# Three blocks per channel-tile pair for the float32 products of a chunked scan among float32r projections

## The chip, the cores and the metric

One Trainium2 chip, one of its cores. The metric is the device time of one execution in microseconds (us). The kernel before was run three times: 1105.64, 1105.64 and 1105.79 us, median 1105.64.

## What is computed

One layer of a streaming encoder on 512 tokens of 1024 numbers: an input layer norm, a mixing layer with two branches (a chunked state-space scan, and top-k attention over shared latents), and a gated convolutional feed-forward layer. The change is in the scan branch. Cut to that, the reference is:

```python
def _ssd_scan(X, a, Bm, Cm):
    ...
    a_cum = jnp.cumsum(a.astype(jnp.float32), axis=-1)
    seg = a_cum[..., :, None] - a_cum[..., None, :]
    decay = jnp.exp(jnp.where(causal, seg, -jnp.inf))
    cb = jnp.einsum('bclgn,bcsgn->bgcls', Cm, Bm)
    y_diag = jnp.einsum('bgecls,bcsgep->bclgep', cb[:, :, None] * decay, X)
    decay_states = jnp.exp(a_cum[..., -1:] - a_cum).transpose(0, 3, 4, 1, 2)
    states = jnp.einsum('bclgn,bclgep->cbgepn', Bm, X * decay_states[..., None])
    ...
    _, prev = lax.scan(step, init, (states, chunk_decay))
    y_off = jnp.einsum('bclgn,cbgepn->bclgep', Cm, prev) * \
        jnp.exp(a_cum).transpose(0, 3, 4, 1, 2)[..., None]
    return (y_diag + y_off).reshape(Bsz, L, H, P)

def _ssd_branch(z, xbc, dt, conv_w, conv_b, dt_bias, A_log, D_skip, norm_g):
    xbc = jax.nn.silu(_causal_dwconv(xbc, conv_w, conv_b))
    ...
    y = _ssd_scan(xs * dt[..., None], dt * A, Bm, Cm)
    y = (y + xs * D_skip[:, None]).reshape(Bsz, L, SSD_INNER)
    v = (y * jax.nn.silu(z)).astype(jnp.float32).reshape(Bsz, L, SSD_GROUPS, SSD_INNER // SSD_GROUPS)
    v = v * lax.rsqrt(jnp.mean(v * v, -1, keepdims=True) + LN_EPS)
    return (v.reshape(Bsz, L, SSD_INNER) * norm_g).astype(z.dtype)
```

The branch has 4 groups of B and C with 128 states each, and 2048 channels. Everything is float32.

## The kernel before

**Two kinds of products on PE (TensorE).** The large projections are exact to about float32 by splitting both factors into a high and a low float32r half: a step is three matmuls, high by high, high by low, low by high, of 128x512 outputs (`mm3`, recorded at L215). A projection of one tile of 128 output channels takes 8 such steps, one per 128 input channels (`steps`, L267), and accumulates in one of three PSUM buffers `acc`. The weights come by DMA on SP's queue into `wraw`; ACT makes `whi` (L188), DVE makes `wlo` (L189). The scan's own products are plain float32 matmuls and transposes of smaller shapes, also recorded at L215 and L218; they write the PSUM banks a, b and c (one buffer each: `pa`, `pb`, `pc` in the profile) and `ptr` (two buffers, `tr_tile`, L111).

**The scan, per group g and channel tile j (128 channels, two heads), L665 to L797.** 

- `ssd_b` transposes B into `bt`, `ssd_cb` multiplies C and B per chunk of 128 tokens into `ptr`, and DVE masks that into `cbm` (both once per group).
- `ssd_x` issues three DMAs (the logs of decay G, two halves of `eaB`), transposes the convolved x into `ptr` (4 transposes), and DVE evicts it twice, as `xdd` (x times dt and decay) and `xd` (x times dt), L702 and L703.
- `ssd_g`, four times per tile, turns G into decays on ACT; `ssd_gm` multiplies G by `cbm` on DVE (L720).
- `ssd_s` makes the states of three chunks (3 products) in bank a or b; ACT and DVE run them through the chunks (`pv`, L735).
- `ssd_y` multiplies C with these states (3 products), DVE multiplies by `eaB` (L747).
- `ssd_d` makes the products within chunks for two tiles (8 products each); DVE (L762), POOL (L763) and the gate add up v.
- After four tiles `ssd_root` sums the squares on PE, `ssd_norm` (four transposes, then DVE at L795) scales v and splits it into `yhi` and `ylo` (L175), the input of the output projection `out_br`.

**The order of the work** around the change is written by hand. `run(projs, items)` (L835) steps through a list of projections and records behind step k the items listed under k; `pair` (L845) makes such a list for two channel tiles from a tuple of steps: x0, x1 (`ssd_x`), s0, s1 (`ssd_s`), y0, y1 (`ssd_y`) and d (`ssd_d`). `AT` (L782) is the usual tuple. The calls from L867 to L884 lay out 8 pairs, named (g, j) here for the first tile j of a pair: (0,0), (0,2), (1,0) and so on to (3,2). In (0,0) and (0,2) they also place `score`, steps of the attention's key selector with two products into `ptr`, evicted by ACT as `rel` (L512). `chain[0]` (L867 to L885) makes each PE instruction depend on the one recorded before, so PE's order is the recorded one. The other engines' orders come from a scheduler by priority; DVE also runs the selector's `max` and `match_replace` on masks (L584, L585) in between.

```python
def ps(tag, bufs=1):
    return ps_.tile([P, T], F32, name="p" + tag, tag=tag, bufs=bufs)
def acc_tile():
    return ps("acc", 3)
def tr_tile():
    return ps("tr", 2)
```

`rms_root` (L252) and `rms_bcast` serve both `ssd_root`/`ssd_norm` and `latents`, where the attention's latents are normed before the scan begins.

Of the kernel before, what the change touches and what calls it, by code (L numbers as in the profile page):

```python
# [57 lines left out]
def tok(i):  # L58
    return slice(i * P, (i + 1) * P)
# [6 lines left out]
def half_of(h):  # L66
    return slice(h * T, (h + 1) * T)
# [3 lines left out]
def block_kernel(ctx, tc, A, out):  # L71
# [16 lines left out]
    def wt(tag, shape, name, dtype=F32):  # L88
        return wk.tile(shape, dtype, name=name, tag=tag, bufs=BUFS[tag])
# [12 lines left out]
    def st(shape, name):  # L102
        return sml.tile(shape, F32, name=name, tag=name)
# [9 lines that stand above are left out]
# [15 lines left out]
    for i in range(NT):  # L128
        t = wt("k4" if i < 2 else "g4", [P, D], "x")
# [35 lines left out]
    def rsqrt_small(src, scale, eps, n, i=0):  # L165

        v = st([P, n], f"rs_v{n}_{i}")
        nc.vector.tensor_scalar(v, src, scale, eps, OP.mult, OP.add)
        y = st([P, n], f"rs_y{n}_{i}")
        last_pow[0] = nc.gpsimd.tensor_tensor(y, v, mhalf[:, :n], OP.pow)  # L170
        return y
# [31 lines left out]
    def w_(name, s, **kw):  # L203
        return wload(A[name][s], **kw)
# [9 lines left out]
    def mm(p, a, b, start, stop):  # L214
        pe(nc.tensor.matmul(p, a, b, start=start, stop=stop).ins)  # L215
# [35 lines left out]

    def rms_root(sqs, n):  # L252

        s4 = ps("b")
        for i in range(NT):
            for j, sq in enumerate(sqs):
                mm(s4[:, i:i + 1], sq[:, tok(i)], ones[:, 0:1], start=j == 0, stop=j == len(sqs) - 1)
        return rsqrt_small(s4[:, :NT], 1.0 / n, EPS, NT)
# [8 lines left out]
    def steps(p, w, rhs, off=0):  # L267
        for k in range(len(rhs)):
            proj(p, w, rhs, off=off, part=(k, k + 1))
            if k < len(rhs) - 1:  # L270
                yield
# [46 lines left out]
    for i, t in enumerate(xt):  # L318
# [5 lines left out]
        v, y, nm = st([P, 1], f"x_v{i}"), st([P, 1], f"x_y{i}"), st([P, 1], f"x_nm{i}")  # L324
# [270 lines left out]
    def conv_silu(dst, p, c):  # L595

        y = wt("cv", [P, T], "cv")
        nc.scalar.activation(y, p, AF.Identity, bias=cwb[:, 96 + c:97 + c], scale=cwb[:, 72 + c:73 + c])
        for k in (2, 1, 0):
            d = 3 - k  # L600
            nc.vector.scalar_tensor_tensor(y[:, d:], p[:, :T - d], cwb[:, 24 * k + c:24 * k + c + 1],  # L601
                                           y[:, d:], OP.mult, OP.add)
        nc.scalar.activation(dst, y, AF.Tanh)
        nc.vector.scalar_tensor_tensor(dst, dst, 1.0, y, OP.add, OP.mult)


    def in_b(g):

        bc = wt("k4", [P, 2, T], "bc")
        sins[g] = {"BT": bc[:, 0], "CT": bc[:, 1], "xs": [], "core": [], "v": []}  # L610
        p = acc_tile()
        yield from steps(p, w_("w_xbc", 16 + g), hT)
        conv_silu(bc[:, 0], p, 16 + g)
        yield

    def in_c(g):

        p = acc_tile()
        yield from steps(p, w_("w_xbc", 20 + g), hT)
        conv_silu(sins[g]["CT"], p, 20 + g)  # L620
        yield

    def in_x(g, j):

        p = acc_tile()
        yield from steps(p, w_("w_xbc", 4 * g + j), hT)
        xj = wt("xs", [P, T], "xs")
        conv_silu(xj, p, 4 * g + j)
        sins[g]["xs"].append(xj)
        yield  # L630

    def in_z(g, j):

        p = acc_tile()
        yield from steps(p, w_("w_z", 4 * g + j), hT)
        zs = wt("m2", [P, T], "zs")
        nc.scalar.activation(zs, p, AF.Tanh, scale=0.5)
        nc.vector.scalar_tensor_tensor(zs, zs, 1.0, p, OP.add, OP.mult)
        sins[g]["z", j] = zs
        ssd_gate(g, j)  # L640
        yield

    def out_br(g, s):

        w = w_("w_br_ssd", 4 * g + s)
        for j in range(2):
            n = 2 * s + j
            p = acc_tile()
            yield from steps(p, w, sins[g]["y"], off=T * j)
            if g == 0:  # L650
                nc.scalar.activation(mssd[:, n], p, AF.Copy)
            else:
                nc.vector.tensor_tensor(mssd[:, n], mssd[:, n], p, OP.add)
            yield
# [94 lines left out]
    def ssd_d(g, js):  # L749

        s_ = sins[g]
        yds = [ps(t) for t in "ca"]
        for j, yd in zip(js, yds):
            xd, xdd, G, eaB, pv = s_["core", j]
            for c in range(NT):
                for h in range(2):
                    mm(yd[h * 64:(h + 1) * 64, tok(c)], xd[:, c, h], G[:, h, c], start=True, stop=True)
        for j, yd in zip(js, yds):
            q = 4 * g + j
            eaB = s_["core", j][3]  # L760
            v = wt("v", [P, T], "v")
            last_v[0] = nc.vector.scalar_tensor_tensor(v, s_["xs"][j], Dv[:, q:q + 1], yd, OP.mult, OP.add)  # L762
            nc.gpsimd.tensor_tensor(v[:, P:], v[:, P:], eaB[:, P:], OP.add)  # L763
            s_["v"].append(v)
            ssd_gate(g, j)

    def ssd_gate(g, j):

        s_ = sins[g]
        if len(s_["v"]) <= j or ("z", j) not in s_:  # L770
            return
        v = s_["v"][j]
        nc.gpsimd.tensor_tensor(v, v, s_["z", j], OP.mult)
        if "ssum" not in s_:
            s_["ssum"] = wt("m2", [P, T], "ssum")
            nc.scalar.activation(s_["ssum"], v, AF.Square)
        else:
            sq = wt("m2", [P, T], "sq")
            nc.scalar.activation(sq, v, AF.Square)
            nc.gpsimd.tensor_tensor(s_["ssum"], s_["ssum"], sq, OP.add)  # L780

    AT = (2, 6, 13, 18, 28, 32, 40)  # L782

    def ssd_root(g):
        sins[g]["r"] = rms_root([sins[g]["ssum"]], 4 * T)
# [49 lines left out]
    def run(projs, items):  # L835

        k = 0
        for p in projs:
            for _ in p:
                for f, *args in items.get(k, ()):  # L840
                    f(*args)
                k += 1
        assert k > max(items), (k, items)

    def pair(g, j, at, more=(), root=11, norm=20):  # L845

        items = {}
        more = [*more]
        if g and not j:
            more += [(root, ssd_root, g - 1), (norm, ssd_norm, g - 1)]  # L850
        x0, x1, s0, s1, y0, y1, d = at
        for n in range(4):
            more += [(s0 + 1 + n, ssd_g, g, j, n), (s1 + 1 + n, ssd_g, g, j + 1, n)]
        more += [(x0, ssd_x, g, j), (x1, ssd_x, g, j + 1), (s0, ssd_s, g, j, "a"), (s1, ssd_s, g, j + 1, "b"),
                 (s1 + 4, ssd_gm, g, j), (s1 + 7, ssd_gm, g, j + 1),
                 (y0, ssd_y, g, j, "a"), (y1, ssd_y, g, j + 1, "b"), (d, ssd_d, g, (j, j + 1))]
        for k, *f in more:
            items.setdefault(k, []).append(f)
        return items

    def scored(*ks):
        return [(k, next, score, None) for k in ks]

    def pin():
# [5 lines left out]
    first_items[44] = [(ssd_cb, 0)]  # L870
    run([in_b(0), in_c(0), out_ga(0), in_x(0, 0), out_ga(1), in_x(0, 1)], first_items)
    run([in_x(0, 2), in_z(0, 0), in_x(0, 3), in_z(0, 1), in_b(1)],
        pair(0, 0, (2, 12, 15, 21, 28, 31, 37), scored(*range(1, 40, 3))))
    run([in_x(1, 0), in_x(1, 1), in_z(0, 2), in_c(1), in_z(0, 3), in_x(1, 2)],
        pair(0, 2, AT, [*scored(3, 5, 7), (21, ssd_b, 1)]))
    for g in (1, 2):
        run([in_x(g, 3), in_b(g + 1), in_z(g, 0), in_z(g, 1), out_br(g - 1, 0), out_br(g - 1, 1), in_c(g + 1)],
            pair(g, 0, AT, [(1, ssd_cb, 1), (18, t5_load), (46, t5_rows)] if g == 1 else ()))
        run([in_x(g + 1, 0), in_z(g, 2), out_br(g - 1, 2), in_x(g + 1, 1), in_z(g, 3), out_br(g - 1, 3),
             in_x(g + 1, 2)], pair(g, 2, AT, [(11, ssd_b, g + 1), (21, ssd_cb, g + 1), (42, pin)]))  # L880
    run([in_x(3, 3), in_z(3, 0), in_z(3, 1), in_z(3, 2), out_br(2, 0)],
        pair(3, 0, (0, 4, 11, 16, 25, 28, 36), [(37, pin)]))
    run([out_br(2, 1), in_z(3, 3), out_br(2, 2), out_br(2, 3)],
        pair(3, 2, (0, 3, 9, 13, 21, 23, 30)))  # L884
    chain[0] = False  # L885


# [201 lines left out]
    for i in range(NT):  # L1089
        for j in range(2):  # L1090
            t = h1[i][:, half_of(j)]
# [36 lines left out]
    for k in range(KR, KW):  # L1128
        d = [wop.tile([P, D], F32R, name=f"wo{k}{j}", tag=f"wo{k}{j}") for j in range(2)]
# [7 lines left out]
    for i in range(NT):  # L1137
# [6 lines left out]
        for j in range(2):  # L1144
            t = h1[i][:, half_of(j)]
# [219 lines left out]
```

## Time and profile before

| | before |
|---|---|
| median of 3 runs | 1105.64 us (1105.64 to 1105.79) |
| the profiled execution | 1106.15 us, span 1104.4 us |
| PE busy | 1088.7 us (99%), 5452 matmuls and transposes |
| DVE, ACT, POOL busy | 772.4 (70%), 478.8 (43%), 168.5 us (15%) |
| mean granted clock of PE | 0.998 |

The profiled execution took 0.5 us more than the median, and its span is 1.75 us shorter than its time. The busy share of PE counts overlapped matmuls: one 128x512 matmul is listed with some 0.39 us, though the next begins 0.23 us after it; the distance of the starts is what one costs. One float32 product is listed as two matmul records (x6 for three products), one transpose as one record. The scan's part of the span is 85 to 430 us.

### The profile page before, as it was taken

What the parts mean: (1) busy time and instruction counts of PE and PEld (TensorE: products, weight loads), DVE (VectorE), ACT (ScalarE), POOL (GpSimd) and SP (SyncE); (2) the same over time, 40 slices, a digit from 0 to 9 for tenths busy, and PEclk for the clock granted to TensorE, in tenths of its full rate; (3) what the DMA queues carried; (4) which work ended last, traced back from release to release, by engine and by line L of the source; (5) the groups of instructions that cost most, each with busy time, mean ns of one, the idle gap of its engine ahead of it and who ended that gap; (6) DMA issues with size and microseconds to landing.
All of it is one profiled execution on the core that took longest, in us unless ns stands there. A gap on an engine that the chain in (4) does not pass through costs nothing.

```text
span 1104.4 us, 14646 instructions
## 1 busy us (share of the span) xinstructions
PE 1088.7 (99%) x5452; PEld 900.1 (82%) x5452; DVE 772.4 (70%) x1402; ACT 478.8 (43%) x825; POOL 168.5 (15%) x183
## 2 busy tenths in 40 slices
PE   8999999999999999999999999999999999999997
PEld 7888888788788888887777778888888888888885
DVE  7667887579967999658899858566656566642227
ACT  6345565453553643255555435115444444432120
POOL 3000203202112023022332460130000000000002
PEclk9999999999999999999999999999999999999999
DMA  7442424554244243322222356402233333232322
GB/s 280 144 152 88 116 77 136 160 178 147 85 129 134 77 134 96 119 93 79 73 72 78 113 195 201 154 1 96 96 97 98 98 104 98 98 96 95 96 96 77
DMA packets 41639, 125.71 MB, mean 114 GB/s; under 512 B 4720, under 2 KB 9120, under 8 KB 41568
## 3 DMA queue, kind: packets, MB, share of 16 engines
q1 hardware_dynamic: 41568, 124.77, 35.2%
q8 instruction: 43, 0.70, 0.3%
q14 instruction: 28, 0.23, 0.1%
HBM read 118.31 MB, written 9.59 MB: 116 GB/s over the span
## 4 chain that ended last, share of the span: by engine, by line
PE 87%; DVE 9%; issue 2%; DMA 1%; ACT 1%; POOL 0%; DVEq 0%
PE pacc L215 52%; PE pc L215 6%; PE pacc L239 6%; PE pb L215 5%; PE pa L215 4%; PE ptr L239 4%; PE ptr L215 2%; PE pb L239 2%; PE pc L239 2%; PE pa L239 2%; DVE wlo L189 2%; DVE mask L585 1%; DVE m L584 1%; PE ptr L218 1%; PE pa L218 1%
## 5 line engine op out<-in xcount | busy, mean ns | idle before, releaser
L189 DVE TENSOR_TENSOR wlo<-wraw,whi 128x1024 fp32r<-128x1024 f32 x159 | 203.2, 1278 | 184.3 <-ACT whi L188 182.9
L188 ACT ACTIVATE whi<-wraw 128x1024 fp32r<-128x1024 f32 x159 | 168.2, 1058 | 235.8 <-PE pacc L215 152.1
L215 PE MATMUL pacc<-hhi,whi 128*128 128x512 f32 (+1 forms) x536 | 219.5, 410 | 0.8 <-ACT hhi L378 0.8
L215 PE MATMUL pacc<-hlo,whi 128*128 128x512 f32 (+1 forms) x536 | 210.5, 393 | 0.8 <-DVE hlo L381 0.8
L215 PE MATMUL pacc<-hhi,wlo 128*128 128x512 f32 (+1 forms) x536 | 209.0, 392 | 0.4 <-DVE wlo L189 0.3
L215 PEld LDWEIGHTS pacc<-hlo,whi 128*128 128x128 f32 (+1 forms) x536 | 100.5, 187 | 24.9 <-DVE hlo L381 2.3
L215 PEld LDWEIGHTS pacc<-hhi,whi 128*128 128x128 f32 (+1 forms) x536 | 100.9, 188 | 19.5 <-issue 1.5
L215 PEld LDWEIGHTS pacc<-hhi,wlo 128*128 128x128 f32 (+1 forms) x536 | 100.8, 188 | 18.2 <-DVE wlo L189 0.7
L215 PE MATMUL pacc<-h1hi,wlo 128*128 128x512 f32 (+1 forms) x216 | 79.0, 366 | 0.0
L215 PE MATMUL pacc<-h1hi,whi 128*128 128x512 f32 (+1 forms) x216 | 78.9, 366 | 0.0
L215 PE MATMUL pacc<-h1lo,whi 128*128 128x512 f32 (+1 forms) x216 | 78.7, 366 | 0.0
L964 POOL TENSOR_TENSOR tm<-mask,toe 128x128 f32<-128x128 f32 (+1 forms) x64 | 44.5, 698 | 162.7 <-DVE mn L975 99.5
L1251 POOL TENSOR_TENSOR rs_y<-rs_v,mhalf 128x1 f32<-128x1 f32 x4 | 4.0, 1004 | 353.8 <-DVE rs_v L1250 349.2
L601 DVE SCALAR_TENSOR_TENSOR cv<-pacc,cwb,cv 128x511 f32<-128x511 f32 (+2 forms) x72 | 53.3, 741 | 0.5
L215 PE MATMUL pacc<-ylo,whi 128*128 128x512 f32 x128 | 50.3, 393 | 1.3 <-DVE ylo L175 1.3
L215 PE MATMUL pacc<-yhi,whi 128*128 128x512 f32 x128 | 51.6, 404 | 0.0
L978 ACT ACTIVATE l<-l,mn 128x128 f32<-128x128 f32 (+1 forms) x64 | 35.7, 558 | 35.5 <-DVE mn L975 34.3
L215 PE MATMUL pacc<-yhi,wlo 128*128 128x512 f32 x128 | 49.9, 390 | 0.0
L763 POOL TENSOR_TENSOR v<-v,eaB 128x384 f32<-128x384 f32 x16 | 17.0, 1080 | 208.5 <-DVE v L762 146.2
L215 PEld LDWEIGHTS pacc<-h1hi,whi 128*128 128x128 f32 x216 | 40.8, 189 | 6.6
L215 PEld LDWEIGHTS pacc<-h1hi,wlo 128*128 128x128 f32 x216 | 40.7, 188 | 6.5
L215 PEld LDWEIGHTS pacc<-h1lo,whi 128*128 128x128 f32 x216 | 40.6, 189 | 6.6
(481 smaller groups left out, 2266.7 us busy)
## 6 DMA issues: line engine op xcount, KB each, us to landing
wraw<-in_w_up_dram SPq DMA_DIRECT2D x44, 512.0 KB, 3.5
wraw<-in_w_xbc_dram SPq DMA_DIRECT2D x24, 512.0 KB, 3.5
wraw<-in_w_down_dram SPq DMA_DIRECT2D x22, 512.0 KB, 3.4
G<-ac_d SPq DMA_DIRECT2D x16, 512.0 KB, 5.6
wraw<-in_w_z_dram SPq DMA_DIRECT2D x16, 512.0 KB, 3.5
wraw<-in_w_br_ssd_dram SPq DMA_DIRECT2D x16, 512.0 KB, 3.6
wraw<-in_w_ga_dram SPq DMA_DIRECT2D x8, 512.0 KB, 3.4
eaB<-ea_d SPq DMA_DIRECT2D x32, 128.0 KB, 5.8
```

The source lines that it names most:

```text
L188: nc.scalar.activation(hi[:, :cols], raw[:, :cols], AF.Copy)
L189: nc.vector.tensor_tensor(lo[:, :cols], raw[:, :cols], hi[:, :cols].bitcast(F32), OP.subtract)
L215: pe(nc.tensor.matmul(p, a, b, start=start, stop=stop).ins)
L218: pe(nc.tensor.transpose(p, a, b).ins)
L239: nc.tensor.matmul(p, x[a][:, tok(i)], w[b][h], start=first and j == 0, stop=last and j == 2)
L584: nc.vector.max(out=m8, in_=S)
L585: nc.vector.match_replace(out=S, in_to_replace=m8, in_values=S, imm_value=-3.4e38)
L601: nc.vector.scalar_tensor_tensor(y[:, d:], p[:, :T - d], cwb[:, 24 * k + c:24 * k + c + 1], y[:, d:], OP.mult, OP.add)
L763: nc.gpsimd.tensor_tensor(v[:, P:], v[:, P:], eaB[:, P:], OP.add)
L964: nc.gpsimd.tensor_tensor(tm[:, :K - f], maskt[i][:, f:], self.toe[:, 2 * P - K + f:], OP.add)
L978: nc.scalar.activation(l[:, :K], l[:, :K], AF.Exp, bias=self.mn[:, ic], scale=-1.0, accum_out=self.sm[:, ic])
L1251: nc.gpsimd.tensor_tensor(y, v, mhalf[:, :1], OP.pow)
```

## The change

`pair` takes three steps instead of seven. At x both tiles' transposes stand together; at s0 the root of the group before (for the first pair of a group) and both tiles' states; at y both tiles' products with the states and the products within chunks. The activations of `ssd_g` and the multiplications `ssd_gm` are placed relative to s0. The calls get new tuples; the transposes and products of B and C and the scores move to other steps, and `ssd_norm` stands 7 steps behind the root. The root's PSUM bank is c instead of b, and the second tile of `ssd_d` is a `ptr` buffer instead of bank a.

```diff
--- before.py
+++ after.py
@@ -251,7 +251,7 @@
 
     def rms_root(sqs, n):
 
-        s4 = ps("b")
+        s4 = ps("c")
         for i in range(NT):
             for j, sq in enumerate(sqs):
                 mm(s4[:, i:i + 1], sq[:, tok(i)], ones[:, 0:1], start=j == 0, stop=j == len(sqs) - 1)
@@ -749,7 +749,7 @@
     def ssd_d(g, js):
 
         s_ = sins[g]
-        yds = [ps(t) for t in "ca"]
+        yds = [ps("c"), tr_tile()]
         for j, yd in zip(js, yds):
             xd, xdd, G, eaB, pv = s_["core", j]
             for c in range(NT):
@@ -779,7 +779,7 @@
             nc.scalar.activation(sq, v, AF.Square)
             nc.gpsimd.tensor_tensor(s_["ssum"], s_["ssum"], sq, OP.add)
 
-    AT = (2, 6, 13, 18, 28, 32, 40)
+    AT = (3, 12, 38)
 
     def ssd_root(g):
         sins[g]["r"] = rms_root([sins[g]["ssum"]], 4 * T)
@@ -842,19 +842,18 @@
                 k += 1
         assert k > max(items), (k, items)
 
-    def pair(g, j, at, more=(), root=11, norm=20):
-
-        items = {}
-        more = [*more]
+    def pair(g, j, at, more=(), norm=None):
+
+        x, s0, y = at
+        items = {x: [(ssd_x, g, j), (ssd_x, g, j + 1)],
+                 s0: [(ssd_s, g, j, "a"), (ssd_s, g, j + 1, "b")],
+                 y: [(ssd_y, g, j, "a"), (ssd_y, g, j + 1, "b"), (ssd_d, g, (j, j + 1))]}
         if g and not j:
-            more += [(root, ssd_root, g - 1), (norm, ssd_norm, g - 1)]
-        x0, x1, s0, s1, y0, y1, d = at
+            items[s0].insert(0, (ssd_root, g - 1))
+            more = [*more, (norm or s0 + 7, ssd_norm, g - 1)]
         for n in range(4):
-            more += [(s0 + 1 + n, ssd_g, g, j, n), (s1 + 1 + n, ssd_g, g, j + 1, n)]
-        more += [(x0, ssd_x, g, j), (x1, ssd_x, g, j + 1), (s0, ssd_s, g, j, "a"), (s1, ssd_s, g, j + 1, "b"),
-                 (s1 + 4, ssd_gm, g, j), (s1 + 7, ssd_gm, g, j + 1),
-                 (y0, ssd_y, g, j, "a"), (y1, ssd_y, g, j + 1, "b"), (d, ssd_d, g, (j, j + 1))]
-        for k, *f in more:
+            more = [*more, (s0 + 1 + n, ssd_g, g, j, n), (s0 + 6 + n, ssd_g, g, j + 1, n)]
+        for k, *f in [*more, (s0 + 9, ssd_gm, g, j), (s0 + 12, ssd_gm, g, j + 1)]:
             items.setdefault(k, []).append(f)
         return items
 
@@ -870,18 +869,18 @@
     first_items[44] = [(ssd_cb, 0)]
     run([in_b(0), in_c(0), out_ga(0), in_x(0, 0), out_ga(1), in_x(0, 1)], first_items)
     run([in_x(0, 2), in_z(0, 0), in_x(0, 3), in_z(0, 1), in_b(1)],
-        pair(0, 0, (2, 12, 15, 21, 28, 31, 37), scored(*range(1, 40, 3))))
+        pair(0, 0, (10, 18, 36), scored(*range(1, 40, 3))))
     run([in_x(1, 0), in_x(1, 1), in_z(0, 2), in_c(1), in_z(0, 3), in_x(1, 2)],
-        pair(0, 2, AT, [*scored(3, 5, 7), (21, ssd_b, 1)]))
+        pair(0, 2, AT, [*scored(4, 6, 8), (38, ssd_b, 1)]))
     for g in (1, 2):
         run([in_x(g, 3), in_b(g + 1), in_z(g, 0), in_z(g, 1), out_br(g - 1, 0), out_br(g - 1, 1), in_c(g + 1)],
-            pair(g, 0, AT, [(1, ssd_cb, 1), (18, t5_load), (46, t5_rows)] if g == 1 else ()))
+            pair(g, 0, AT, [(3, ssd_cb, 1), (18, t5_load), (46, t5_rows)] if g == 1 else ()))
         run([in_x(g + 1, 0), in_z(g, 2), out_br(g - 1, 2), in_x(g + 1, 1), in_z(g, 3), out_br(g - 1, 3),
-             in_x(g + 1, 2)], pair(g, 2, AT, [(11, ssd_b, g + 1), (21, ssd_cb, g + 1), (42, pin)]))
+             in_x(g + 1, 2)], pair(g, 2, AT, [(12, ssd_b, g + 1), (38, ssd_cb, g + 1), (42, pin)]))
     run([in_x(3, 3), in_z(3, 0), in_z(3, 1), in_z(3, 2), out_br(2, 0)],
-        pair(3, 0, (0, 4, 11, 16, 25, 28, 36), [(37, pin)]))
+        pair(3, 0, (1, 10, 34), [(37, pin)]))
     run([out_br(2, 1), in_z(3, 3), out_br(2, 2), out_br(2, 3)],
-        pair(3, 2, (0, 3, 9, 13, 21, 23, 30)))
+        pair(3, 2, (1, 9, 29)))
     chain[0] = False
```

PE's order in (0,0), of the second place on (xs are x's tiles, khi, klo and qi the selector's factors, hhi, hlo, whi and wlo the projection's halves). Before, around x0:

```order
L215 MATMUL ptr_940<-khi_630,qi_382 128x384
L215 MATMUL ptr_940<-klo_631,qi_382 128x384
L215 MATMUL pacc_927<-hhi_125,whi_930 128x512
L215 MATMUL pacc_927<-hhi_125,wlo_931 128x512
L215 MATMUL pacc_927<-hlo_126,whi_930 128x512
L218 MATMUL ptr_954<-ident_102,xs_788 128x128 x4
L215 MATMUL pacc_927<-hhi_125,whi_930 128x512
L215 MATMUL pacc_927<-hhi_125,wlo_931 128x512
```

and with the change, around the block of x0 and x1:

```order
L215 MATMUL pacc_984<-hhi_125,wlo_988 128x512
L215 MATMUL pacc_984<-hlo_126,whi_987 128x512
L218 MATMUL ptr_1005<-ident_102,xs_788 128x128 x4
L218 MATMUL ptr_1019<-ident_102,xs_912 128x128 x4
L215 MATMUL ptr_1028<-khi_630,qi_382 128x384
L215 MATMUL ptr_1028<-klo_631,qi_382 128x384
L215 MATMUL pacc_984<-hhi_125,whi_987 128x512
L215 MATMUL pacc_984<-hhi_125,wlo_988 128x512
```

The score `ptr_1028` now stands behind two tiles of transposes with no step between, where it stood behind one with a step between.

PE's order in (2,0), at the products of the first two tiles of group 2 (bc is C, pv the states). Before, around `ssd_d`:

```order
L215 MATMUL pacc_2734<-yhi_2615,wlo_2731 128x512
L215 MATMUL pacc_2734<-ylo_2616,whi_2730 128x512
L215 MATMUL pc_2738<-G_2458,xd_2468 64x128 x8
L215 MATMUL pa_2739<-G_2484,xd_2494 64x128 x8
L215 MATMUL pacc_2734<-yhi_2615,whi_2730 128x512
L215 MATMUL pacc_2734<-yhi_2615,wlo_2731 128x512
```

and with the change:

```order
L215 MATMUL pacc_2704<-yhi_2612,wlo_2687 128x512
L215 MATMUL pacc_2704<-ylo_2613,whi_2686 128x512
L215 MATMUL pa_2714<-bc_1733,pv_2545 128x128 x3
L215 MATMUL pb_2719<-bc_1733,pv_2555 128x128 x3
L215 MATMUL pc_2724<-G_2461,xd_2471 64x128 x8
L215 MATMUL ptr_2725<-G_2475,xd_2485 64x128 x8
L215 MATMUL pacc_2704<-yhi_2612,whi_2686 128x512
L215 MATMUL pacc_2704<-yhi_2612,wlo_2687 128x512
L215 MATMUL pacc_2704<-ylo_2613,whi_2686 128x512
```

The products with states, which stood at two places of their own, are now ahead of those within chunks, and the second tile's go to `ptr`.

DVE's order in (2,0), ahead of the output projection of group 1 (v and ylo are group 1's, G, pv and eaB group 2's). Before:

```order
L175 TENSOR_TENSOR ylo_2616<-v_1983,yhi_2615 128x512
L189 TENSOR_TENSOR wlo_2731<-wraw_2728,whi_2730 128x1024
L638 SCALAR_TENSOR_TENSOR zs_2646<-zs_2646,pacc_2571 128x512
L735 SCALAR_TENSOR_TENSOR pv_2596<-pv_2596,cd_136,pb_2592 128x64
L175 TENSOR_TENSOR ylo_2616<-v_1989,yhi_2615 128x512
L735 SCALAR_TENSOR_TENSOR pv_2596<-pv_2596,cd_136,pb_2592 128x64
L585 MATCH_REPLACE mask1_128<-m8_137,mask1_128 128x256
L747 TENSOR_TENSOR eaB_2460<-pa_2672,eaB_2460 128x384
L720 TENSOR_TENSOR G_2484<-G_2484,cbm_2238 128x1024
L601 SCALAR_TENSOR_TENSOR cv_2562<-pacc_2510,cwb_465,cv_2562 128x509
L175 TENSOR_TENSOR ylo_2616<-v_2365,yhi_2615 128x512
L175 TENSOR_TENSOR ylo_2616<-v_2372,yhi_2615 128x512
```

and with the change:

```order
L189 TENSOR_TENSOR wlo_2687<-wraw_2684,whi_2686 128x1024
L601 SCALAR_TENSOR_TENSOR cv_2574<-pacc_2510,cwb_465,cv_2574 128x511
L720 TENSOR_TENSOR G_2461<-G_2461,cbm_2357 128x1024
L720 TENSOR_TENSOR G_2475<-G_2475,cbm_2357 128x1024
L175 TENSOR_TENSOR ylo_2613<-v_1969,yhi_2612 128x512
L175 TENSOR_TENSOR ylo_2613<-v_1975,yhi_2612 128x512
L601 SCALAR_TENSOR_TENSOR cv_2574<-pacc_2510,cwb_465,cv_2574 128x510
L189 TENSOR_TENSOR wlo_2762<-wraw_2759,whi_2761 128x1024
L638 SCALAR_TENSOR_TENSOR zs_2646<-zs_2646,pacc_2583 128x512
L175 TENSOR_TENSOR ylo_2613<-v_2342,yhi_2612 128x512
L175 TENSOR_TENSOR ylo_2613<-v_2349,yhi_2612 128x512
```

Both G products now stand ahead of the first ylo, and no pv or eaB row stands between the four.

## Rows read from the trace of the kernel before

**Rows 1.** The page: busy time and instructions, granted clock in 40 slices, chain of waits.

```profile
PE 1088.7 (99%) x5452; PEld 900.1 (82%) x5452; DVE 772.4 (70%) x1402; ACT 478.8 (43%) x825; POOL 168.5 (15%) x183
...
PEclk9999999999999999999999999999999999999999
...
PE 87%; DVE 9%; issue 2%; DMA 1%; ACT 1%; POOL 0%; DVEq 0%
```

**Rows 2.** Table of stretches: length, busy PE, PEld, DVE, ACT, POOL, granted clock, DMA.

```profile
85.00:160.00 75.00, 75.00 (x397) 62.97 (x396) 60.14 (x98) 45.29 (x92) 7.81 (x7) 1.00 0.31 95
160.00:250.00 90.00, 89.77 (x485) 73.99 (x484) 60.75 (x93) 45.42 (x85) 15.52 (x13) 1.00 0.51 156
250.00:345.00 95.00, 93.79 (x509) 77.31 (x510) 76.44 (x145) 46.03 (x84) 15.33 (x13) 1.00 0.35 111
345.00:430.00 85.00, 85.00 (x474) 70.70 (x470) 83.42 (x161) 38.69 (x74) 25.97 (x21) 1.00 0.36 112
```

**Rows 3.** PE's timeline in (2,0): start, duration, instruction, count [idle before].

```profile
268.75 0.39 PE L215 MATMUL pacc<-hlo,whi 128*128 128x512 f32 x1
268.98 0.60 PE L218 MATMUL ptr<-ident,xs 128*128 128x128 f32 x4
269.34 0.49 PE L215 MATMUL pacc<-hhi,whi 128*128 128x512 f32 x1
269.66 0.39 PE L215 MATMUL pacc<-hhi,wlo 128*128 128x512 f32 x1
...
272.20 0.39 PE L215 MATMUL pacc<-hhi,whi 128*128 128x512 f32 x1
```

**Rows 4.** PE's timeline before the scan, transposes of keys and of B.

```profile
73.35 0.60 PE L496 MATMUL ptr<-ident,kn 128*128 128x128 f32 x4
73.78 0.60 PE L218 MATMUL ptr<-ident,bc 128*128 128x128 f32 x4
74.14 0.48 PE L215 MATMUL pacc<-hhi,whi 128*128 128x512 f32 x1
...
76.95 0.39 PE L215 MATMUL pacc<-hhi,whi 128*128 128x512 f32 x1
```

**Rows 5.** PE's timeline, two blocks of states and of products with them, in (2,0) and (3,0).

```profile
287.28 0.83 PE L215 MATMUL pa<-bc,pv 128*128 128x128 f32 x6
...
366.46 0.91 PE L215 MATMUL pa<-xdd,bt 128*128 128x128 f32 x6
```

**Rows 6.** PE's timeline, products within chunks of two tiles, in (2,0).

```profile
298.79 1.09 PE L215 MATMUL pc<-G,xd 128*64 128x128 f32 x16
...
300.69 0.50 PE L215 MATMUL pacc<-yhi,whi 128*128 128x512 f32 x1
301.03 0.40 PE L215 MATMUL pacc<-yhi,wlo 128*128 128x512 f32 x1
```

**Rows 7.** DVE's timeline ahead of evictions in (0,0), (0,2) and (1,0).

```profile
92.52 1.23 DVE L189 TENSOR_TENSOR wlo<-wraw,whi 128x1024 fp32r<-128x1024 f32 x1 [1.51 <-ACT whi L188]
...
95.04 0.55 DVE L702 TENSOR_TENSOR xdd<-ptr,dts 128x384 f32<-128x384 f32 x1
95.51 0.68 DVE L703 TENSOR_TENSOR xd<-ptr,dt 128x512 f32<-128x512 f32 x1
...
131.12 1.92 DVE L189 TENSOR_TENSOR wlo<-wraw,whi 128x1024 fp32r<-128x1024 f32 x1 [1.88 <-ACT whi L188]
...
171.73 1.80 DVE L189 TENSOR_TENSOR wlo<-wraw,whi 128x1024 fp32r<-128x1024 f32 x1 [4.42 <-ACT whi L188]
```

**Rows 8.** PE's timeline at the waits for ylo, in (1,0) and (2,0).

```profile
197.87 0.39 PE L215 MATMUL pacc<-yhi,wlo 128*128 128x512 f32 x1
198.49 0.50 PE L215 MATMUL pacc<-ylo,whi 128*128 128x512 f32 x1 [0.23 <-DVE ylo L175]
...
292.77 0.39 PE L215 MATMUL pacc<-yhi,wlo 128*128 128x512 f32 x1
294.25 0.50 PE L215 MATMUL pacc<-ylo,whi 128*128 128x512 f32 x1 [1.09 <-DVE ylo L175]
```

## The prediction, made before the changed kernel ran

> **What bounds the kernel now.** I read the page first. PE is busy for 1088.7 of 1104.4 us, the granted clock stands in the top tenth in all 40 slices, and the chain of work that ended last is 87% PE [rows 1]. So nearly every microsecond that PE saves is one of the kernel, and every one that PE waits is lost. Next I read the stretches that hold the scan, 85 to 430 us: PE runs through them with at most 1.2 us of idle time in each, at a granted clock of 1.00 (the 2.4 GHz level), while DVE is busy for 80, 67, 80 and 98% of them [rows 2]. A change to PE's order there can win only what PE's own sequence costs, and it can lose by making PE wait for an engine that has a queue of its own. Then I read PE's timeline around single blocks of float32 products.
>
> **What a block costs [rows 3].** In the middle of a projection a step starts 0.23 us (227 ns) after the one ahead (268.75, 268.98). Behind four transposes of `xs` the first step takes 0.32 us to the next one (269.34 to 269.66). From the block's start at 268.98 to the thirteenth step behind it at 272.20 are 3.22 us; twelve intervals of 227 ns are 2.72, so the block cost 0.49 to 0.50. Inside a run of transposes four of them take 0.43 (73.35 to 73.78) [rows 4]. Being a block of its own thus costs some 0.05 us. In the one place where two blocks of four transposes already stand together, the same count (73.35 to 76.95, thirteenth step again: 3.60 less 2.72) gives 0.88 for both, against 0.98 for two single ones: 0.09 to 0.10 saved by one merger, the upper bound. For the lower one I take a place where two kinds stand together: six records of `pa<-xdd,bt` last 0.91 us behind the sums of `ssum`, while six of `pa<-bc,pv` alone last 0.83 [rows 5]. A change of kind inside a block costs 0.08, almost the 0.09 of the first step behind a block, so a merger can be worth as little as 0.01.
>
> **How many blocks go.** Each of eight pairs has seven places now and three afterwards: 32 fewer. The three root products that had a place of their own join the states (3), and the transposes and products of B and C join other places: one in (1,0), one in (0,2), two in each of (1,2) and (2,2), 6 in all. In (0,0) three of the old places stood beside a score of the selector already and only one of the new ones does, so 2 fewer are saved there. Sum 39. At 0.05 us each PE saves **1.9 us**, with bounds of 0.4 (39 x 0.01) and 3.5 (39 x 0.09). I take 0.05 because most mergers are of the kinds that it was read from.
>
> **What does not change price.** The products within chunks keep their own entry and exit: 32 records from 298.79 to 300.69, the first step behind taking 0.34 [rows 6]. The number of PE's products, the DMAs on SP's queue (each `ssd_x` issues one G and two eaB loads; x1's now go out with x0's, further ahead of their use), the evictions and the activations all stay. The bank of the root products, b to c, and the second bank of `ssd_d`, a to one of the two `ptr` buffers, cost nothing by themselves: the other products on these banks have been evicted by then, steps before. The 16 relu activations per pair move by a step or two; ACT, busy for 46 to 60% there [rows 2], covers them, and without that cover the exponent of G would come later by as much as the queue is behind.
>
> **What the change adds: a third tile of `ptr`.** That pool has two buffers. A block that holds x0, x1 and one thing more that needs `ptr` stops until DVE has evicted x0, and PE being in order, all projection steps behind it stop too. It happens at three places: in (0,0) at step 10, where a score of the selector follows the eight transposes; in (0,2), where a score follows one step later; in (1,0), where the products of C and B stand in the same block. The eviction of x0 is xdd and xd, together 1.15 us as DVE runs them (95.04 to 96.19) [rows 7]. x0's four transposes start and end within 0.60 us [rows 3], so the third tile comes free at 0.60 + 1.15 + some 0.1 until PE is told = 1.85 us after the block's start. PE arrives there after eight transposes, 0.79 us (73.35 to 74.14) [rows 4]. The wait is at least 1.05 us where the third tile stands in the block, and 1.05 less 0.68 for three steps, some 0.35, in (0,2). On top comes what DVE is at when x0 is ready: a `wlo` of 1.23 to 1.92 us stands just ahead of these evictions now [rows 7], and in (0,2) the new order puts a `cv`, of half a `wlo` or so, between xdd and xd. I add 0.45 us at (0,0), 0.8 at (0,2) and 0.15 at (1,0), estimates from parts of that queue: waits of 1.5, 1.15 and 1.2 us. The transposes of the keys and of B stand together with another tile as well, some 0.2 us. Sum **4.0 us**; bounds 2.5 (least waits) and 6.5 (a whole `wlo` ahead at two places).
>
> **What stays: the wait for ylo.** Before the output projection of a group PE waits for the low halves of y. The largest such wait is between 292.77 and 294.25, 1.48 us instead of 0.23, another at 198.49, 0.62 (from 197.87) instead of 0.23: 1.6 us together [rows 8]. The change takes two pv rows and two eaB products out of DVE's queue ahead of the last ylo, but places both G products ahead of the first. Summed in the new order by the durations of the trace, the last ylo ends about when it did. I cost this at 0, between a gain of 1.6 and a loss of 0.5.
>
> **Sum.** Against the profiled execution of 1106.15 us: -1.9 + 4.0 + 0 = +2.1, so 1108.25; the median of the three runs is 0.5 lower, 1105.64, which gives **1107.7 us**. A difference of 0.2% is 2.2 us, about what a measurement of this kernel tells from nothing, so the forecast lies at the edge of what can be seen: a saving spread over 39 places is given back at three.
>
> **A rule to weigh.** The clock stood at 1.00 in every stretch, with float32 blocks of 1.9 us among the steps [rows 2, 6]; the longest new blocks hold 0.6 + 0.6 + 1.9 us of products, and up to eight transposes stand together. The Trainium skill, "TensorE: Matmul & The Clock Gate", section "Part 4: PE-mode transpose", says that transposes don't count as PE activity in the way that matmuls do, so that the clock gate doesn't open for them. By that rule longer blocks are what could cost the clock, which is rival D.
>
> **Rivals.**
> A. *DVE is behind at all three places.* If a whole `wlo` is in the way each time, a wait is some 2.3 us (1.05 + 1.25), the new waits cost 3 x 2.3 + 0.2 = 7.1, and the time is 1105.6 - 1.9 + 7.1 = 1110.8. For it: DVE is busy for 80% of the first stretch [rows 2]. Against: it has idle gaps of 1.5 to 4.4 us ahead of those `wlo` [rows 7], so it starts without a backlog. 0.18.
> B. *The ylo waits go.* If the rows that leave DVE's queue were what made ylo late, 1.6 us come back: 1105.6 - 1.9 + 4.0 - 1.6 = 1106.1. For it: they stood right ahead of it. Against: the G products, 1.2 us each as a `wlo` is, move ahead. 0.2.
> C. *The other side: blocks are dearer than I price them.* If a merger is worth the 0.09 of rows 4 the saving is 3.5; with the least waits, 2.5, and ylo's gone, 1.6, the time is 1105.6 - 3.5 + 2.5 - 1.6 = 1103.0, faster by 0.24%. It decides from a price of 0.08 per merger on. Against: the mixed kinds of rows 5. 0.13.
> D. *The clock falls in the long blocks.* If the granted clock fell to its lower level, 1.2 GHz, for the eight blocks of 3.1 us, each would take twice as long: 8 x 3.1 = 25 us, some 1130. Rows 2 and 6 show nothing of it in blocks of 1.9 us. 0.02.
> E. *The change doesn't do what it says.* PE takes its instructions in the order in which they are recorded here, so the blocks do merge: nil.
>
> **How the numbers follow.** The forecast has 0.47, A 0.18, B 0.2, C 0.13, D 0.02. The range reaches up to A and down to where half of C's way is gone: 1104.0 to 1110.8, which also holds the forecast with either bound of its waits (1106.2 to 1110.2). From the median, faster by more than 2.2 us means below 1103.4: C and the tails beside it, 0.15. Slower by more than 2.2 us means above 1107.85: A, D and some 0.2 of the forecast, 0.4. The rest, 0.45, is within 0.2%.
>
> **What would show it.** In the changed profile the first step behind a merged block still takes 0.31 to 0.34 us, but there are 39 fewer of these. Idle time of PE ended by DVE's xd should appear at the transposes' places in (0,0), (0,2) and (1,0), near 100, 133 and 173 us, about 1 to 1.5 us each. The ylo wait near 294 us should stand within 1 us of what it was, and the granted clock at 1.00 in each stretch. The prediction is wrong if the three waits are missing, if ylo's wait is gone, or if the steps behind the new blocks are slower than 0.34 us.

## The result, and the profile after

The changed kernel takes **1114.45 us** (median of 6 runs, 1113.06 to 1115.78) against 1105.66 (6 runs, 1105.62 to 1105.79): 1.0078 times as long, 95% interval 1.0068 to 1.0088. That is slower by 8.8 us, above the range of 1104.0 to 1110.8. The profiled execution took 1114.50 us with a span of 1112.8, against 1106.15 and 1104.4.

The page of the changed kernel, to be read beside [rows 1]:

```profile
PE 1089.7 (98%) x5452; PEld 903.9 (81%) x5452; DVE 774.6 (70%) x1402; ACT 478.1 (43%) x825; POOL 172.4 (15%) x183
...
PE 89%; DVE 6%; issue 2%; ACT 1%; POOL 1%; DMA 0%; DVEq 0%; POOLq 0%
```

PE is busy for 1.0 us more than before, so 7.4 of the 8.4 us of longer span are idle time. The table of stretches, with the columns of [rows 2], says where:

```profile
85.00:160.00 75.00, 72.50 (x378) 60.92 (x377) 57.89 (x94) 44.88 (x91) 8.23 (x7) 1.00 0.29 95
160.00:250.00 90.00, 85.19 (x457) 70.35 (x456) 59.21 (x90) 43.97 (x84) 16.37 (x13) 0.98 0.48 145
250.00:345.00 95.00, 91.91 (x494) 77.03 (x493) 75.81 (x143) 43.64 (x81) 17.53 (x13) 1.00 0.35 111
345.00:430.00 85.00, 85.00 (x492) 72.00 (x492) 81.13 (x157) 38.63 (x73) 19.88 (x16) 1.00 0.39 118
```

PE is idle for 2.5, 4.8 and 3.1 us in three stretches that had 0, 0.2 and 1.2. In the second of these the granted clock is 0.98.

PE's timeline at the three places of the third `ptr` tile, (0,0), (0,2) and (1,0):

```profile
100.08 1.04 PE L218 MATMUL ptr<-ident,xs 128*128 128x128 f32 x8
102.58 0.41 PE L215 MATMUL ptr<-khi,qi 128*128 128x384 f32 x1 [1.46 <-DVE xd L703]
...
136.81 0.47 PE L215 MATMUL ptr<-khi,qi 128*128 128x512 f32 x1 [1.03 <-DVE xd L703]
...
175.47 1.03 PE L218 MATMUL ptr<-ident,xs 128*128 128x128 f32 x8
178.01 1.13 PE L215 MATMUL ptr<-bc 128*128 128x128 f32 x8 [1.50 <-DVE xd L703]
```

These are the waits that the prediction named: 1.46, 1.03 and 1.50 us of idle time, each ended by DVE's xd. DVE's timeline at the first shows what stands ahead of that eviction:

```profile
98.95 1.23 DVE L189 TENSOR_TENSOR wlo<-wraw,whi 128x1024 fp32r<-128x1024 f32 x1 [0.93 <-ACT whi L188]
100.10 0.74 DVE L601 SCALAR_TENSOR_TENSOR cv<-pacc,cwb,cv 128x511 f32<-128x511 f32 x1
100.76 0.61 DVE L516 SCALAR_TENSOR_TENSOR mask<-rel,sp,mask 128x384 f32<-128x384 f32 x1
101.28 0.55 DVE L702 TENSOR_TENSOR xdd<-ptr,dts 128x384 f32<-128x384 f32 x1
101.75 0.68 DVE L703 TENSOR_TENSOR xd<-ptr,dt 128x512 f32<-128x512 f32 x1
```

The transposes begin at 100.08; x0's are done some 0.6 us later, and xdd starts at 101.28, behind `wlo`, `cv` and `mask`.

PE's timeline at the start of the output projections in (1,0) and (2,0), which answers to [rows 8], and at a projection behind one in (1,2):

```profile
200.53 0.39 PE L215 MATMUL pacc<-hlo,whi 128*128 128x512 f32 x1
203.81 0.80 PE L215 MATMUL pacc<-yhi,whi 128*128 128x512 f32 x1 [2.89 <-DVE zs L638]
...
245.94 0.50 PE L215 MATMUL pacc<-hhi,whi 128*128 128x512 f32 x1 [0.42 <-ACT mssd L651]
...
300.86 0.50 PE L215 MATMUL pacc<-yhi,whi 128*128 128x512 f32 x1 [3.09 <-DVE zs L638]
```

Two waits of 2.9 and 3.1 us that nobody had named, and they are ended by `zs`, not by ylo. `zs` (L638) is the gate of a projection `in_z` and the last reader of its accumulator in PSUM; the first product of the output projection, `pacc<-yhi,whi`, needs that buffer. DVE's timeline from the norm to this `zs` in (1,0):

```profile
192.77 2.72 DVE L795 SCALAR_TENSOR_TENSOR v<-v,ngh,pc 128x512 f32<-128x512 f32 x4 [2.02 <-PE pc L218]
195.41 1.22 DVE L189 TENSOR_TENSOR wlo<-wraw,whi 128x1024 fp32r<-128x1024 f32 x1
196.55 0.75 DVE L601 SCALAR_TENSOR_TENSOR cv<-pacc,cwb,cv 128x511 f32<-128x511 f32 x1
197.21 2.35 DVE L720 TENSOR_TENSOR G<-G,cbm 128x1024 f32<-128x1024 f32 x2
199.48 1.29 DVE L175 TENSOR_TENSOR ylo<-v,yhi 128x512 fp32r<-128x512 f32 x2
200.68 0.75 DVE L601 SCALAR_TENSOR_TENSOR cv<-pacc,cwb,cv 128x510 f32<-128x510 f32 x1
201.34 0.69 DVE L175 TENSOR_TENSOR ylo<-v,yhi 128x512 fp32r<-128x512 f32 x1
201.94 1.22 DVE L189 TENSOR_TENSOR wlo<-wraw,whi 128x1024 fp32r<-128x1024 f32 x1
203.07 0.68 DVE L638 SCALAR_TENSOR_TENSOR zs<-zs,pacc 128x512 f32<-128x512 f32 x1
```

From 192.77 on DVE runs without a break, behind an idle time of 2.0 us ahead of it, and `zs` stands near the end of that bunch, with one ylo still behind it. In the kernel before the same `zs` stood ahead of the second G product and of all ylo:

```profile
196.03 0.68 DVE L638 SCALAR_TENSOR_TENSOR zs<-zs,pacc 128x512 f32<-128x512 f32 x1
196.62 1.22 DVE L720 TENSOR_TENSOR G<-G,cbm 128x1024 f32<-128x1024 f32 x1
197.76 1.28 DVE L175 TENSOR_TENSOR ylo<-v,yhi 128x512 fp32r<-128x512 f32 x2
```

In (2,0) `zs` was on time by less than 0.1 us even in the kernel before. Its row on DVE and the first product of the output projection on PE:

```profile
289.28 0.68 DVE L638 SCALAR_TENSOR_TENSOR zs<-zs,pacc 128x512 f32<-128x512 f32 x1
...
290.04 0.47 PE L215 MATMUL pacc<-yhi,whi 128*128 128x512 f32 x1
```

The accumulator can only have been that of `zs` there: the last readers of the other two, a `cv` and a second `zs`, ended at 293.6 and 296.5. In the changed kernel PE could have started at about 297.6 there (its last product ahead starts at 297.39), and the row on DVE is

```profile
300.13 0.68 DVE L638 SCALAR_TENSOR_TENSOR zs<-zs,pacc 128x512 f32<-128x512 f32 x1
```

The granted clock just behind the wait in (1,0), each row 1 us (columns as in [rows 2]):

```profile
203.00:204.00 1.00, 0.19 (x1) 0.19 (x2) 1.00 (x3) 0.00 (x0) 0.00 (x0) 0.90 0.00 0
204.00:205.00 1.00, 1.00 (x3) 0.82 (x4) 1.00 (x3) 0.00 (x0) 0.00 (x0) 0.50 0.82 197
...
206.00:207.00 1.00, 1.00 (x4) 0.72 (x4) 1.00 (x3) 0.00 (x0) 0.00 (x0) 0.50 0.05 21
...
208.00:209.00 1.00, 1.00 (x6) 0.81 (x5) 0.00 (x0) 0.56 (x1) 0.00 (x0) 1.00 0.91 373
```

From the end of the wait to 207.2 PE has half its clock, the 1.2 GHz level: the starts of eight of the projection's matmuls stand mostly 0.43 us apart instead of 0.23, which costs some 1.5 us in all. Behind the equally long wait in (2,0) the clock stays at 1.00.

**The account.** The same matmuls of the projections stand in both traces, in the same order. The first of them behind a pair starts later than before by:

| behind pair | (0,0) | (0,2) | (1,0) | (1,2) | (2,0) | (2,2) | (3,0) | (3,2) |
|---|---|---|---|---|---|---|---|---|
| us later | 1.49 | 2.31 | 8.04 | 8.51 | 10.00 | 9.74 | 9.30 | 9.07 |

By the starts (the distance between the starts of two neighbouring matmuls, less what it is without a wait), the three `ptr` waits cost 1.71, 1.16 (1.28 less 0.12 before) and 1.74, together 4.6 us. The delays at the accumulators cost 4.3 us more than before in (1,0), with the 1.5 of the clock, 1.8 more in (2,0) and 0.2 less in (3,0), 5.9 us at the output projections; with 0.7 in (1,2) they make 6.6 us. What is left in each pair is 0.2 to 0.35 us faster, 2.2 in all, and 0.7 come back between the scan and the end of PE's work, most of it at two places, near 444 and 627 us of the kernel before. 4.6 + 6.6 - 2.2 - 0.7 = 8.3.

### The profile page after: what moved, and what is told of

It reads as the page before. It is cut to its first block, busy times and chain, and to the rows that moved or that the text cites. A ratio compares the mean times of both kernels' runs of the same rounds, so it can differ in the third digit from the quotient of the medians.

```text
span 1112.8 us, 14632 instructions
## 1 busy us (share of the span) xinstructions
PE 1089.7 (98%) x5452; PEld 903.9 (81%) x5452; DVE 774.6 (70%) x1402; ACT 478.1 (43%) x825; POOL 172.4 (15%) x183
## 4 chain that ended last, share of the span: by engine, by line
PE 89%; DVE 6%; issue 2%; ACT 1%; POOL 1%; DMA 0%; DVEq 0%; POOLq 0%
PE pacc L215 54%; PE pc L215 7%; PE pacc L239 6%; PE pb L215 5%; PE pa L215 4%; PE ptr L239 4%; PE ptr L215 3%; PE pb L239 2%; PE pc L239 2%; PE pa L239 2%; DVE wlo L189 1%; PE pa L218 1%; PE ptr L218 1%; PE pb L218 1%; DVE pt L993 1%
## 5 line engine op out<-in xcount | busy, mean ns | idle before, releaser
L215 PE MATMUL pacc<-hhi,whi 128*128 128x512 f32 (+1 forms) x536 | 216.4, 404 | 1.2 <-ACT hhi L378 0.8
```

## The experiments

**e1_g_behind_zs: the order on DVE.** NOSYNC dependencies, which here only fix the order within DVE's queue, put both G products of (1,0) and (2,0) behind `zs`.

```diff
+        if g in (1, 2) and j < 2:
+            tc.add_manual_dep(i.ins, sins[g]["zi", 0].name, NOSYNC, reason="order")
```

(`i` is the G product, `zi` the instruction that writes zs; the G products are recorded at s0 + 12 and s0 + 15 there.)

> The changed kernel with one order turned round on DVE: in (1,0) and (2,0) both G products stand behind zs of the projection in_z(g,0), not ahead of it. Theory Z (the output projection's first product waits for the accumulator buffer that zs empties, and zs is queued behind both G products): the two waits of 2.9 and 3.1 us shrink by the 2.3 us of the two G products each, and the granted clock of 0.5 behind the first of them does not come: 1114.4 - 4.6 - 1.5 = 1108.3 us, runs within 0.5 us of each other. Rival Q (DVE simply has too much to do ahead of the output projection, the order in which it does so does not matter): the wait is ended by ylo instead of zs and is as long, 1113 to 1115 us.

Measured: 1111.29 us (1111.20 to 1111.84), 3.2 us back of the 6.1 expected. PE's timeline at the two output projections:

```profile
202.01 0.47 PE L215 MATMUL pacc<-yhi,whi 128*128 128x512 f32 x1 [0.77 <-DVE cv L601]
...
205.38 0.50 PE L215 MATMUL pacc<-ylo,whi 128*128 128x512 f32 x1 [0.60 <-DVE ylo L175]
...
296.07 0.50 PE L215 MATMUL pacc<-yhi,whi 128*128 128x512 f32 x1 [0.81 <-DVE zs L638]
...
298.94 0.50 PE L215 MATMUL pacc<-ylo,whi 128*128 128x512 f32 x1 [0.76 <-DVE ylo L175]
```

Neither theory was right as it stood. The two long waits are gone and the clock stays up, but each has become two of 0.6 to 0.8 us, for `cv` or `zs` (a buffer again) and for ylo. By the starts (1,0) is 2.8 us shorter than in the changed kernel, 1.5 of it the clock, and (2,0) 1.1 us. So the order matters. That the amount of work that DVE has there limits the rest is argued from these new waits and is not shown by this run alone.

**e2_thirds_apart: the third tile alone.**

```diff
-        pair(0, 0, (10, 18, 36), scored(*range(1, 40, 3))))
+        pair(0, 0, (10, 18, 36), scored(1, 3, 5, 7, *range(14, 39, 3))))
-        pair(0, 2, AT, [*scored(4, 6, 8), (38, ssd_b, 1)]))
+        pair(0, 2, AT, [*scored(8, 10, 14), (38, ssd_b, 1)]))
-            pair(g, 0, AT, [(3, ssd_cb, 1), (18, t5_load), (46, t5_rows)] if g == 1 else ()))
+            pair(g, 0, AT, [(7, ssd_cb, 1), (18, t5_load), (46, t5_rows)] if g == 1 else ()))
```

> The changed kernel with the third ptr tile moved away from the transposes of x: in (0,0) and (0,2) the scores and in (1,0) the products of C and B stand at least four steps behind that block. Theory T (the third tile waits for DVE's eviction of the first, 4.0 us by the idle time in front of the three, 4.9 us by the starts): 1114.4 - 4.9 + 0.2 for the blocks that stand alone again = 1109.7 us. Rival B (DVE is behind at these places, so that the next thing that needs it waits instead): at most half of it comes back, 1112 us or more.

Measured: 1111.63 us (1110.99 to 1113.80), 2.8 us back in the median. The trace says more than the median: (0,0) and (0,2) together are now 0.7 us faster than in the kernel before, no `ptr` wait is left in the list of PE's waits, and the two waits for zs stand unchanged (6.0 us together). In this execution the clock fell at the one in (2,0), for 13 matmuls, 2.7 us. Without that fall and the one in the changed kernel's profile, the first matmul behind the scan starts 4.7 us earlier than in the changed kernel, as theory T says. The median misses T's 1109.7 by 1.9 us. The four runs differ in the mean granted clock as well: 1111.0 and 1111.1 us at 0.996, 1112.2 at 0.995, 1113.8 at 0.994.

**e3_both: both repairs,** with the last ylo ahead of G as well.

> The changed kernel with both: the third tiles apart, and both G products in (1,0) and (2,0) behind zs and behind the last ylo. Theories T and Z together: the three blocks per pair then show what they save by themselves, 2.6 us by the starts of the steps in the changed kernel's trace, plus most of the 2.3 us that the kernel before waits at the same places: 1105.7 - 2.5 - 1.5 = 1101.7 us (1100.8 to 1103.2), no clock below 1.00 in these stretches. Rival M (long float32 blocks cost something themselves): not below 1105 us.

Measured: 1105.23 us (1104.89 to 1105.87, 10 runs), 0.9994 times before, interval 0.9985 to 1.0004: 9.2 us back, but not the gain. The time alone is what rival M said (not below 1105); what speaks against M is where PE waits, and e6 below, which keeps the blocks. By the starts PE still waits 0.9 us in (1,0), 0.7 in (1,2) and 2.5 in (2,0).

**e4_before_g_behind: the order alone, in the kernel before.** The second tile's G product is put behind `zs` and the last ylo.

> The kernel before with the order alone: in (1,0) and (2,0) the second tile's G product stands behind zs and the last ylo on DVE. Theory Z: the waits of the kernel before at these places (0.5 and 1.85 us by the starts) shrink by up to the 1.2 us of that product each: 1105.7 - 1.5 = 1104.2 us (1103.7 to 1105.0). Rival Q: 1105.5 to 1106 us, unchanged.

Measured: 1105.66 us (1105.13 to 1106.39, 10 runs), unchanged, as rival Q said. In the trace the matmuls behind the scan do start 1.7 us earlier, and the last matmul 2.0 us earlier, but the span is only 0.9 shorter: the last store took 1.1 us longer to land (below). So in the profiled execution the order helped PE as theory Z says, and the time doesn't show it. Whether the later landing is what hid it in the other nine runs is not shown.

**e5_norm_early: the start of the bunch,** the changed kernel with one number.

```diff
-            pair(g, 0, AT, [(3, ssd_cb, 1), (18, t5_load), (46, t5_rows)] if g == 1 else ()))
+            pair(g, 0, AT, [(3, ssd_cb, 1), (18, t5_load), (46, t5_rows)] if g == 1 else (), norm=15))
```

> The changed kernel with the norm of the group before recorded 3 steps behind the root in (1,0) and (2,0) instead of 7; third tiles and G products as in the change. Theory W (what delays zs is DVE's work, bunched behind the norm: v, ylo, both G, wlo and cv, some 11 us with 3 us of idle time just ahead of it; the order inside the bunch matters only as far as something can go behind zs): the bunch starts up to 2.7 us earlier, the waits of 2.9 and 3.1 us fall to 0.3 to 0.8, the clock stays at 1.00 there: 1114.4 - 4.8 - 1.5 = 1108.1 us (1107.3 to 1109.5). Rival Z (only the G products in front of zs count): the wait stays at 2.5 us or more, 1113 us.

Measured: 1112.12 us (1111.81 to 1113.11), 2.3 us back of the 6.3 expected. Theory W was right in (1,0), wrong in (2,0). The timelines of PE and DVE at the output projection in (1,0), and of PE in (2,0):

```profile
201.66 0.39 PE L215 MATMUL pacc<-yhi,whi 128*128 128x512 f32 x1
...
199.74 0.74 DVE L601 SCALAR_TENSOR_TENSOR cv<-pacc,cwb,cv 128x509 f32<-128x509 f32 x1
...
203.27 0.68 DVE L638 SCALAR_TENSOR_TENSOR zs<-zs,pacc 128x512 f32<-128x512 f32 x1
...
297.10 0.50 PE L215 MATMUL pacc<-yhi,whi 128*128 128x512 f32 x1 [3.22 <-DVE zs L638]
```

In (1,0) the output projection starts at 201.66 without a wait while `zs` has not begun, so it has got another of the three accumulators; the last `cv`, which reads one of them, was done at 200.5. In (2,0) it still gets that of `zs`, and waits 3.2 us for it. So it counts which buffer the program hands out next and where its last reader stands in DVE's queue, and an earlier start of the bunch alone is not enough. Why the buffer differs between the two places stays open.

**e6_both_norm_early, e7_exp_first, e8_mssd_on_dve.** e6 is e3 with `norm=15`. e7 adds that on ACT the first tile's exponent goes ahead of the second tile's eight relu. e8 is e6 with

```diff
-                nc.scalar.activation(mssd[:, n], p, AF.Copy)
+                nc.vector.tensor_copy(mssd[:, n], p)
```

> Third tiles apart, G products behind zs and ylo, and the norm 3 steps behind the root in (1,0) and (2,0). Theory W: what e3_both still waits there (0.9 us in (1,0), 2.5 us in (2,0) by the starts) goes but for some 0.3: 1105.2 - 3.0 = 1102.2 us (1101.5 to 1103.2), faster than the kernel before by 0.3%. Rival (another accumulator release is late next, as with ylo or cv): 1104 to 1105 us.

> As e6_both_norm_early, and on ACT the exponent of a pair's first G stands ahead of the second tile's eight relu activations in every pair. Theory W: nothing waits for the first G any more, so within 0.3 us of e6_both_norm_early. Rival (ACT's bunch of 16 activations and two exponents delays releases of PSUM buffers): the wait of 0.6 us in (1,2), ended by ACT's copy into mssd, gets longer by up to 1 us, since an exponent moves ahead of it.

> As e6_both_norm_early, and the first group's output projections are copied out of PSUM by DVE instead of ACT. If ACT's bunch of activations is what makes the projection wait 0.6 us in (1,2), that wait goes: 0.7 us less than e6_both_norm_early, 1101.5 us. If DVE is as late there: no change.

Measured: e6 1102.46 us (0.9971 times before, 0.9959 to 0.9983); e7 1102.92; e8 1101.70 (0.9962, 0.9947 to 0.9977). In e6 the waits in (1,0) are gone and 0.2 us is left in (2,0). There, too, the output projection has another accumulator, and `zs` has left the path: in (2,0) PE starts before `zs` does.

```profile
288.76 0.47 PE L215 MATMUL pacc<-yhi,whi 128*128 128x512 f32 x1
...
289.87 0.68 DVE L638 SCALAR_TENSOR_TENSOR zs<-zs,pacc 128x512 f32<-128x512 f32 x1
```

In (1,0) it starts at 196.57, and `zs` ends at 196.7. In e3 both projections had started right behind `zs` (197.13 behind 197.07, 290.35 behind 290.29). So e6 changes the start of the bunch and the buffer at once, and how much each is worth is not separated.

e8 takes away the 0.7 us of (1,2), so the place of the copy `mssd` in ACT's queue was the cause there. In the changed kernel ACT runs without a break from 236.91 to that copy at 245.30, through both tiles' sixteen relu, an exponent and a `whi`. In e8 0.4 us of idle time for `cv` come in (2,0). e7, 0.5 us above e6 where 0.3 was expected, did not lengthen the wait in (1,2), as its rival had it; it brought one of 0.70 us for `cv` in (2,0).

**e9_before_repaired and e10_all_again: what the three blocks are worth.**

> The kernel before, its seven places kept, with the same repairs as e8_mssd_on_dve where they apply: the second G product behind zs and the last ylo, the norm 4 steps behind the root instead of 9 in (1,0) and (2,0), the first group's copies out of PSUM on DVE. By the accounts so far the waits of 2.3 us at the output projections go or nearly go and the 39 blocks stay: 1105.6 - 2.0 = 1103.6 us (1103.0 to 1104.6). Then three blocks per pair are worth 2 to 2.6 us by themselves, against e10_all_again. Rival (the merged blocks are worth nothing, all of the gain of e8_mssd_on_dve is the repairs): 1101.7 us.

> The kernel of e8_mssd_on_dve once more, on the same chip as e9_before_repaired: 1101.7 us (1101.4 to 1102.2).

Measured: e9 1104.70 us (0.9991, 0.9982 to 0.9999), e10 1101.81 (0.9965, 0.9952 to 0.9979), 2.9 us apart. e9 misses its range by 0.1 us, and its rival (1101.7) by 3.0. It still has a wait of 1.1 us for zs in (2,0), where its order came out worse than in e4; e10 has one of 0.4 us. By the starts, with the waits of both taken out, the pairs of e10 are 2.4 us faster than those of e9 (0.2 to 0.5 each), with 45 blocks in the scan instead of 81: the value of the merged blocks by themselves. The kernel of e8 and e10 is the fastest here, 3.9 us faster than the one before.

## Why the prediction was wrong

- **What bounds the kernel:** right. Nearly all of the difference is idle time of PE, 7.4 of 8.4 us, and in the scan each such wait is ended by DVE or ACT, engines with queues of their own. The rest, 1.0 us more of busy time, comes with the half clock behind one of these waits, which the prediction had not tied to waiting.
- **The price of a block** ([rows 3], [rows 4]): right. PE's timeline of the changed kernel in (2,0), from two tiles' transposes to the thirteenth matmul of the projection behind (the prediction calls such a single matmul a step there):

```profile
274.96 1.03 PE L218 MATMUL ptr<-ident,xs 128*128 128x128 f32 x8
275.75 0.48 PE L215 MATMUL pacc<-hhi,whi 128*128 128x512 f32 x1
...
278.58 0.39 PE L215 MATMUL pacc<-hhi,whi 128*128 128x512 f32 x1
```

3.62 us less 2.72 are 0.90 for both, against 0.98 for two single blocks. Over all pairs 2.2 us were saved. Between the projections' matmuls of the scan PE's trace has 81 blocks before and 43 with the change, 38 fewer where the prediction had 39; that makes 0.06 us each, where it had 0.05 and 1.9 in all.
- **"What the change adds: a third tile of `ptr`":** right in place, kind and releaser. Counted as the prediction counts, by the starts, the three cost 4.6 us (4.0 us of idle time) against 3.85 predicted; the 0.2 us for the keys' and B's transposes did not come. e2's trace confirms it.
- **"What stays: the wait for ylo ... I cost this at 0, between a gain of 1.6 and a loss of 0.5":** this is the step that failed. The term put at 0 measured 5.9 us, 1.5 of it the clock. What it says of ylo came out: the last ylo ends 3.4 us behind the end of the projection ahead, where it was 2.9, in (1,0), and 4.2 instead of 4.6 in (2,0). But I summed DVE's new queue as far as ylo and asked only when ylo ends. In the same queue stands `zs`, the last reader of the accumulator that the output projection takes. In (1,0) it had moved from ahead of the second G and of all ylo to behind both G and three ylo. The order rows of (2,0) ahead of the prediction show the like: from ahead of the second G to behind both G and the second ylo. "What does not change price" had named the banks a, b, c and `ptr` and left out the third pool, `acc`. e1 shows that the order of G and `zs` accounts for 3.9 of the 6.1 us of (1,0) and (2,0), the clock's 1.5 among them; e5 that the rest depends on which buffer is handed out; e6 that the wait goes when G and the last ylo are in another order and the norm is earlier, with another buffer handed out in both places.
- **ACT "covers" its activations:** not quite. Sixteen relu in one bunch made its copy out of `acc` in (1,2) late, 0.7 us, which e8 removes. It is the same omission: this copy is the last reader of an accumulator.
- **The rivals:** B and C needed the ylo wait to go; it did, and a longer one for `zs` took its place. The lower end of the range, 1104.0, is called half of C's way; half of the way from the median to 1103.0 is 1104.3. A had DVE's queue as the danger, at the wrong three places. D had the clock fall in the long blocks. It fell, which cost 1.5 us, but behind idle time; the longest new block, 4.2 us of float32 products at the end of (1,2) (the prediction's longest had 3.1; the products of C and B join them there), ran at 1.00, as the stretch shows:

```profile
256.30:260.50 4.20, 4.20 (x52) 3.89 (x51) 3.11 (x6) 0.63 (x1) 0.78 (x1) 1.00 0.25 89
```

The rule of the Trainium skill ("TensorE: Matmul & The Clock Gate", "Part 4: PE-mode transpose") that was weighed there shows in no run here.

## What to carry to other kernels

When work is merged into larger blocks on the bounding engine, list every pool of PSUM that this engine takes buffers from, and for each the last reader of the buffer and its place in its engine's new queue; the inputs of the next product are only half of what it waits for. Merging bunches the followers as well: a pair of blocks that fed ACT and DVE at two times now feeds them at once, and whatever is queued behind that bunch comes late. The gain of 2.2 to 2.4 us was real and small, and one release in the wrong place, 4.3 us in (1,0) with the clock behind it, cost more than all mergers gave.

## What was not expected of the hardware

- **The clock behind a pause of PE.** Five waits of 2.9 to 3.2 us were profiled (two in the changed kernel, two in e2, one in e5). At three of them the granted clock fell to 0.5 for 8 to 13 matmuls, 1.5 to 2.7 us in all: 0.9 us before the end of the wait in e2, at its end in the changed kernel, 1.1 us behind it in e5. At the other two it stayed at 1.00, and so it did all through the scan in the nine other profiles, whose waits there are 1.5 us at most. Of the changed kernel's six runs the two shortest, 1113.1 and 1113.3 us, have a mean granted clock of 0.998, the four others, 1114.4 to 1115.8 us, 0.996. The clock is not all that spreads the runs: those of e8 lie within 0.13 us, but those of the kernel before, with no long wait either, spread over 1.15 us in nineteen runs (1105.41 to 1106.56). Why some pauses are followed by the lower clock and others of the same length are not stays open.
- **The last store.** From SP's last issue to the end of the span are 2.7 us in the kernel before and 3.8 in e4:

```profile
1100.71 0.99 SPq L1260 DMA_DIRECT2D out_dram<-h  x2
```

```profile
1098.72 1.00 SPq L1265 DMA_DIRECT2D out_dram<-h  x2
```

With spans of 1104.4 and 1103.5 us, the end came 0.9 earlier though the store was issued 2.0 earlier. From issue to landing the last store took 2.0 us in ten of the twelve profiles and 3.1 in e2 and e4; why stays open.
